# A hybrid Fourier, attention and expert layer on one core: each expert weight chunk rounded and subtracted whole, not in two halves

## The chip, the core and the metric

The kernel runs on one core of a Trainium2 chip. The metric is the device time of one execution in microseconds, of the median of the runs.

## The reference

One layer over a sequence of 1024 tokens of width 1024, all in float32. A mixing sub-layer (Fourier branch, grouped attention, gates, output projection) is followed by a routed feed-forward sub-layer with 32 experts, of which each token takes four. The change lies in this second one:

```python
def expert_block(args):
    e, rows = args
    xb = xf[rows]
    h = xb @ w_gate_up[e] + b_gate_up[e]
    gate, up = h[:, :D_EXPERT], h[:, D_EXPERT:]
    gate = jnp.minimum(gate, SWIGLU_LIMIT)
    up = jnp.clip(up, -SWIGLU_LIMIT, SWIGLU_LIMIT)
    act = (up + 1.0) * gate * jax.nn.sigmoid(SWIGLU_ALPHA * gate)
    return act @ w_down[e] + b_down[e]
```

`w_gate_up[e]` is 1024 x 2048 and `w_down[e]` 1024 x 1024, so the 32 experts' weights are 402 MB, each read once.

## The kernel before

TensorE multiplies float32 numbers here as pairs of rounded ones. A weight `w` becomes `whi`, the rounded value, and `wlo`, what the rounding left over (`w - whi`); the activations (`xTa`, `xTb`, `aTa`, `aTb`) are split in the same way. A product is then the sum of three matmuls (high by high, high by low, low by high; L141 to L143, L1140 to L1144), or of two where both parts of the activation stand side by side (L1184 and L1185, L1219 and L1220). ACT rounds (L147) and DVE subtracts (L148), both in the helper `split` (L145).

After the first sub-layer, the router and the placing of tokens comes the expert stage, from about 1090 to 2790 us of the span. The experts are ranked by their load; the fourteen fullest (up to 416 tokens) form lane a, which keeps weights stationary and puts tokens in the columns (`cols`, PSUM tile `psg`, and `psd` on the way down); the others (up to 128 or 64 tokens) form lane b, which keeps tokens stationary (`rows`, PSUM tile `psr`). `moe_plan` (L64) writes the order in which steps of the two lanes take turns, by estimated times. In lane b two chunks make one step pair, so the usual turn on TensorE is two short chunks of b and one longer of a.

Each expert has 12 chunks of weights, 1 MB each: eight of gate and up, four of down; 32 x 12 = 384 chunks. `load_chunk` (L1009) gets one: SP issues one or two DMAs into `wraw` (128 x 2048), and then `split` makes `whi` and `wlo`. Each of the three tiles has three buffers (pool `pew`, L1045), and a `Stream` (L1069) calls `load_chunk` two chunks ahead. A `wraw` buffer is free for the next load when DVE has subtracted; `whi` and `wlo` are free when TensorE has done with the chunk. The order of a chunk in `wraw` is by rows of the weight, so the first half of the tile holds the rows that the first matmuls of the chunk use, and these can start when the first half is split.

DVE and ACT have more to do in the stage: they take results out of PSUM (`gu`, `gur`, `xya`, `xyb`), compute the gated unit (`sgg`, `av`) and split activations (`aTa`, `aTb`, `xTa`, `xTb`). Every engine works its instructions in a fixed order. A scheduler in the build settles this order, by times that it assumes for each instruction; so a change of sizes also moves instructions.

Of the kernel before, what the change touches and what calls it, by code (L numbers as in the profile page):

```python
# [37 lines left out]
CAPS = [416, 320, 288, 288, 256, 256, 240, 208, 208, 192, 192, 160, 160, 160] + 7 * [128] + 11 * [64]  # L38

RANK_AT = 6  # L40
HALVES = [(0, 4), (4, 8)]
N_BIG = sum(n > P for n in CAPS)
LANE_A = [9, 0, 4, 1, 5, 2, 6, 3, 7, 8, 10, 11, 12, 13]
LANE_B = list(range(NE - 1, N_BIG - 1, -1))
# [62 lines left out]
def layer_kernel(ctx, tc, x, c, w_ada, b_ada, w_in, q_norm_g, k_norm_g, w_fourier, w_attn_o, w_out,  # L107
# [37 lines left out]
    def split(raw, hi, lo, lo_eng=None):  # L145

        act.activation(hi, raw, AF.Copy)  # L147
        (lo_eng or vec).tensor_tensor(lo, raw, f32(hi), op=ALU.subtract)  # L148
        return hi, lo
# [859 lines left out]
    def load_chunk(pl, wgu, wdn, i, wide=True, after=None):  # L1009
# [15 lines left out]
        with tc.issue_after(after.ins) if after else nullcontext():  # L1025
            for a, b in HALVES:
                split(raw[:, a:b, :], hi[:, a:b, :], lo[:, a:b, :])
# [456 lines left out]
```

## Time and profile before

| what | value |
|---|---|
| median of 3 runs | 2825.12 us (2825.11 to 2833.14) |
| the profiled execution | 2837.53 us, its span 2835.8 us |
| PE busy in the span | 2547.5 us (90%) |
| DVE busy | 2103.1 us (74%) |
| ACT busy | 1415.0 us (50%) |
| moved by DMA | 557.04 MB, mean 196 GB/s |

The profile is of one execution. Busy times of PE are of pipelined matmuls, so a busy PE is not PE at its peak; the idle time between them is what other engines and the clock leave to be won. PEld is the load of weights into TensorE, which goes ahead of the matmul; a wait for weights is seen there first.

### The profile page before, as it was taken

What the parts mean: (1) busy time and instruction counts of PE and PEld (TensorE: products, weight loads), DVE (VectorE), ACT (ScalarE), POOL (GpSimd) and SP (SyncE); (2) the same over time, 40 slices, a digit from 0 to 9 for tenths busy, and PEclk for the clock granted to TensorE, in tenths of its full rate; (3) what the DMA queues carried; (4) which work ended last, traced back from release to release, by engine and by line L of the source; (5) the groups of instructions that cost most, each with busy time, mean ns of one, the idle gap of its engine ahead of it and who ended that gap; (6) DMA issues with size and microseconds to landing.
All of it is one profiled execution on the core that took longest, in us unless ns stands there. A gap on an engine that the chain in (4) does not pass through costs nothing. (4 is left out here: it accounts for less than half of the span.)

```text
span 2835.8 us, 43042 instructions
## 1 busy us (share of the span) xinstructions
PE 2547.5 (90%) x15948; PEld 2308.4 (81%) x15948; DVE 2103.1 (74%) x3676; ACT 1415.0 (50%) x2174; POOL 412.2 (15%) x311
## 2 busy tenths in 40 slices
PE   6999999899999845889999999998999999998991
PEld 5888899799888834789889888986898888897881
DVE  7543338777755775878688888878897888887885
ACT  3411122466621533646466566656664665665662
POOL 3100002111031542000200010111101000120003
PEclk9999999999999957899999999999999999999996
DMA  6164420000054236767888798978988898988774
GB/s 227 57 195 152 152 66 16 16 1 1 1 186 134 68 112 215 252 212 244 244 272 281 249 293 268 299 228 267 309 264 258 265 295 272 301 274 267 240 252 151
DMA packets 466439, 557.04 MB, mean 196 GB/s; under 512 B 26377, under 2 KB 404689, under 8 KB 466177
## 3 DMA queue, kind: packets, MB, share of 16 engines
q1 hardware_dynamic: 448672, 494.41, 53.2%
q0 software_dynamic: 16464, 55.44, 7.4%
q10 hardware_dynamic: 1088, 4.39, 0.5%
q8 instruction: 127, 2.08, 0.3%
q14 instruction: 88, 0.71, 0.1%
HBM read 512.90 MB, written 42.62 MB: 196 GB/s over the span
## 5 line engine op out<-in xcount | busy, mean ns | idle before, releaser
L148 DVE TENSOR_TENSOR wlo<-wraw,whi 128x1024 fp32r<-128x1024 f32 x768 | 910.5, 1217 | 215.9 <-ACT whi L147 207.0
L147 ACT ACTIVATE whi<-wraw 128x1024 fp32r<-128x1024 f32 x768 | 768.5, 1051 | 462.5 <-DMA wraw<-in_w_gate_up_dram 155.3
L1144 PE MATMUL psg<-xTa,wlo 128*128 128x160 f32 (+7 forms) x1792 | 470.9, 278 | 1.6 <-DVE wlo L148 1.5
L1144 PEld LDWEIGHTS psg<-xTa,wlo 128*128 128x128 f32 x1792 | 342.5, 194 | 5.4 <-DVE wlo L148 3.3
L1140 PE MATMUL psg<-xTa,whi 128*128 128x320 f32 (+3 forms) x1024 | 308.7, 369 | 14.7 <-ACT whi L147 11.2
L141 PE MATMUL psd<-whi,aTa 128*128 128x256 f32 (+2 forms) x768 | 221.1, 292 | 27.8 <-ACT aTa L1168 14.9
L1142 PE MATMUL psg<-xTa,whi 128*128 128x256 f32 (+3 forms) x768 | 231.6, 306 | 8.7 <-ACT whi L147 7.5
L1143 PE MATMUL psg<-xTa,whi 128*128 128x256 f32 (+3 forms) x768 | 230.7, 304 | 0.0
L143 PE MATMUL psd<-whi,aTa 128*128 128x256 f32 (+2 forms) x768 | 217.3, 288 | 2.8 <-DVE aTa L1169 2.8
L142 PE MATMUL psd<-wlo,aTa 128*128 128x256 f32 (+2 forms) x768 | 218.1, 287 | 0.2 <-DVE wlo L148 0.2
L1140 PEld LDWEIGHTS psg<-xTa,whi 128*128 128x128 f32 x1024 | 197.0, 195 | 24.7 <-ACT whi L147 13.7
L141 PEld LDWEIGHTS psd<-whi,aTa 128*128 128x128 f32 (+2 forms) x768 | 146.1, 191 | 36.3 <-ACT aTa L1168 18.0
L1142 PEld LDWEIGHTS psg<-xTa,whi 128*128 128x128 f32 x768 | 146.5, 191 | 12.4 <-ACT whi L147 8.7
L1006 POOL DMA_INDIRECT acc_d<-xya,tab x33 | 60.9, 1847 | 649.7 <-DVE xya L1231 544.0
L143 PEld LDWEIGHTS psd<-whi,aTa 128*128 128x128 f32 (+2 forms) x768 | 145.6, 191 | 4.2 <-DVE aTa L1169 3.5
L142 PEld LDWEIGHTS psd<-wlo,aTa 128*128 128x128 f32 (+2 forms) x768 | 146.4, 191 | 1.6 <-DVE wlo L148 0.8
L1143 PEld LDWEIGHTS psg<-xTa,whi 128*128 128x128 f32 x768 | 146.7, 191 | 1.4
L1184 PE MATMUL psr<-whi,xTb 128*128 128x512 f32 x352 | 143.4, 407 | 4.3 <-ACT whi L147 4.2
L1185 PE MATMUL psr<-wlo,xTb 128*128 128x512 f32 x352 | 144.6, 411 | 2.0 <-DVE wlo L148 2.0
L147 ACT ACTIVATE wh<-wraw 128x1024 fp32r<-128x1024 f32 (+1 forms) x35 | 48.2, 1377 | 154.6 <-PE psg L206 93.1
L152 ACT ACTIVATE pth<-pst 128x512 fp32r<-128x512 f32 x128 | 75.0, 598 | 86.6 <-PE pst L632 85.3
L141 PE MATMUL pz<-wh,uh 128*128 128x256 f32 x384 | 110.5, 288 | 2.4 <-DVE mrow L480 2.4
(471 smaller groups left out, 6450.1 us busy)
## 6 DMA issues: line engine op xcount, KB each, us to landing
wraw<-in_w_gate_up_dram SPq DMA_DIRECT2D x512, 512.0 KB, 5.3
wraw<-in_w_down_dram SPq DMA_DIRECT2D x128, 1024.0 KB, 5.3
wa<-in_w_ada_dram SPq DMA_DIRECT2D x24, 1024.0 KB, 7.3
wraw<-in_w_in_dram SPq DMA_DIRECT2D x13, 1024.0 KB, 6.2
xs<-in_x_dram SPq DMA_DIRECT2D x8, 512.0 KB, 8.7
m_d<-sgm POOLq DMA_DIRECT2D x8, 512.0 KB, 5.7
sa_d<-sgm POOLq DMA_DIRECT2D x8, 512.0 KB, 3.2
wraw<-in_w_attn_o_dram SPq DMA_DIRECT2D x8, 512.0 KB, 3.6
```

The costliest lines, as they stand in the source:

```text
L141: pe_.matmul(o, lh, rh, start=start, stop=False)
L142: pe_.matmul(o, lh, rl, start=False, stop=False)
L143: pe_.matmul(o, ll, rh, start=False, stop=stop)
L147: act.activation(hi, raw, AF.Copy)
L148: (lo_eng or vec).tensor_tensor(lo, raw, f32(hi), op=ALU.subtract)
L152: act.activation(hi, ps, AF.Copy)
L1140: pe_.matmul(ps[:, :2 * n], wh[:, k, cs], xT[:, 4 * h + k, :, :], start=first, stop=False)
L1142: pe_.matmul(ps[:, :n], wh[:, k, cs], xh, start=first, stop=False)
L1143: pe_.matmul(ps[:, :n], wh[:, k, cs], xl, start=False, stop=False)
L1144: pe_.matmul(ps[:, :n], wl[:, k, cs], xh, start=False, stop=last)
L1184: pe_.matmul(o, xk, wh[:, k, :], start=False, stop=False)
L1185: pe_.matmul(o, xk, wl[:, k, :], start=False, stop=last)
```

## The change

The list of parts in which `load_chunk` splits a chunk has one entry instead of two. ACT rounds the whole chunk by one instruction, and DVE subtracts it by one.

```diff
-HALVES = [(0, 4), (4, 8)]
+HALVES = [(0, 8)]
```

It is used in one place (L1026):

```python
for a, b in HALVES:
    split(raw[:, a:b, :], hi[:, a:b, :], lo[:, a:b, :])
```

No tile, buffer, DMA or matmul is added or taken away. The scheduler gives another order, though. On DVE, in the middle of the stage (expert of lane a with 256 tokens, one of b with 64), before; `wlo_15436` and `wlo_15461` are two chunks of lane b, `gur` and `av1` belong to the gated unit of lane b, `sgg`, `aTa` and `gu` to lane a:

```order
L1194 TENSOR_TENSOR gur_15449<-psr_15402,gur_15449 64x512
L148 TENSOR_TENSOR wlo_15436<-wraw_15432,whi_15435 128x1024
L1038 TENSOR_SCALAR gur_15449<-gur_15449 64x256
L1039 TENSOR_SCALAR gur_15449<-gur_15449 64x256
L148 TENSOR_TENSOR wlo_15436<-wraw_15432,whi_15435 128x1024
L1162 TENSOR_TENSOR sgg_15392<-gu_15389,sgg_15392 128x256
L1041 SCALAR_TENSOR_TENSOR gur_15449<-gur_15449 64x256
L148 TENSOR_TENSOR wlo_15461<-wraw_15457,whi_15460 128x1024 x2
L1042 TENSOR_TENSOR av1_9761<-av1_9761,gur_15449 64x256
L1169 TENSOR_TENSOR aTa_15212<-sgg_15392,aTa_15212 128x2x128
```

The same place after, where `wlo_15436` is called `wlo_15186` and `wlo_15461` is `wlo_15209`:

```order
L1194 TENSOR_TENSOR gur_15197<-psr_15154,gur_15197 64x512
L148 TENSOR_TENSOR wlo_15186<-wraw_15182,whi_15185 128x2048
L1162 TENSOR_TENSOR sgg_15144<-gu_15141,sgg_15144 128x256
L1038 TENSOR_SCALAR gur_15197<-gur_15197 64x256
L1039 TENSOR_SCALAR gur_15197<-gur_15197 64x256
L1041 SCALAR_TENSOR_TENSOR gur_15197<-gur_15197 64x256
L148 TENSOR_TENSOR wlo_15209<-wraw_15205,whi_15208 128x2048
L1169 TENSOR_TENSOR aTa_14972<-sgg_15144,aTa_14972 128x2x128
L1042 TENSOR_TENSOR av1_9761<-av1_9761,gur_15197 64x256
```

The two steps on `gur` that stood between the halves of a chunk now stand behind the whole chunk's subtraction, with the step on `sgg` ahead of them. In the whole program 120 chunks had other DVE work between their halves, 167 instructions; now none has.

On PE, some 10 us later, before; `psr` is lane b's sum (its chunk is `whi_15569`, `wlo_15570`), `psg` lane a's (its chunk is `whi_15647`, `wlo_15648`), and L1205 is a transpose of lane b's activations:

```order
L1184 MATMUL psr_15643<-whi_15569,xTb_15168 128x512
L1185 MATMUL psr_15643<-wlo_15570,xTb_15168 128x512
L1184 MATMUL psr_15643<-whi_15569,xTb_15168 128x512
L1185 MATMUL psr_15643<-wlo_15570,xTb_15168 128x512
L1184 MATMUL psr_15643<-whi_15569,xTb_15168 128x512
L1205 MATMUL ptr_15869<-ident_63,av1_9761 128x128 x2
L1142 MATMUL psg_15696<-xTa_14756,whi_15647 128x256
L1143 MATMUL psg_15696<-xTa_14756,whi_15647 128x256
L1142 MATMUL psg_15697<-xTa_14756,whi_15647 128x256
L1143 MATMUL psg_15697<-xTa_14756,whi_15647 128x256
L1185 MATMUL psr_15643<-wlo_15570,xTb_15168 128x512
L1184 MATMUL psr_15643<-whi_15569,xTb_15168 128x512
```

The same place after, where the chunk of lane b is `whi_15311`, `wlo_15312` and that of lane a `whi_15387`, `wlo_15388`:

```order
L1184 MATMUL psr_15383<-whi_15311,xTb_14930 128x512
L1142 MATMUL psg_15430<-xTa_14530,whi_15387 128x256
L1143 MATMUL psg_15430<-xTa_14530,whi_15387 128x256
L1142 MATMUL psg_15431<-xTa_14530,whi_15387 128x256
L1143 MATMUL psg_15431<-xTa_14530,whi_15387 128x256
L1185 MATMUL psr_15383<-wlo_15312,xTb_14930 128x512
L1184 MATMUL psr_15383<-whi_15311,xTb_14930 128x512
L1185 MATMUL psr_15383<-wlo_15312,xTb_14930 128x512
```

Four matmuls of lane a that read its `whi` have moved from the chunk's middle to behind its first matmul on `whi`, and lane b's first matmul on `wlo` comes after them; the transpose has moved to a later place.

## Rows read from the trace of the kernel before

**Rows 1.** The page, busy us (share of the span) and instructions of each engine.

```profile
PE 2547.5 (90%) x15948; PEld 2308.4 (81%) x15948; DVE 2103.1 (74%) x3676; ACT 1415.0 (50%) x2174; POOL 412.2 (15%) x311
```

**Rows 2.** Busy time by window, the expert stage; columns in the first row.

```profile
core 0: us, PE busy (x) PEld busy (x) DVE busy (x) ACT busy (x) POOL busy (x), PEclk, DMA share, GB/s
1090.00:2790.00 1700.00, 1573.14 (x9912) 1439.52 (x9912) 1393.39 (x2286) 1015.50 (x1521) 173.69 (x98) 0.97 0.82 261
```

**Rows 3.** Waits of the weight loads, expert stage: us in total, times, longest us.

```profile
PEld psg L1140 <- ACT whi L147: 13.7, 7, 5.2
...
PEld psr L142 <- DVE wlo L148: 6.0, 8, 1.1
...
PEld psr L1184 <- ACT whi L147: 5.9, 5, 3.0
...
PEld psd L142 <- DVE wlo L148: 0.8, 2, 0.5
```

**Rows 4.** Waits of the weight loads for other results, same view.

```profile
PEld psd L141 <- ACT aTa L1168: 18.0, 10, 5.4
...
PEld psr L1180 <- DVE xyb L1231: 0.8, 1, 0.8
```

**Rows 5.** Groups of instructions: busy us, mean ns of one, idle before; whole span.

```profile
L148 DVE TENSOR_TENSOR wlo<-wraw,whi 128x1024 fp32r<-128x1024 f32 x768 | 910.5, 1217 | 215.9 <-ACT whi L147 207.0
L147 ACT ACTIVATE whi<-wraw 128x1024 fp32r<-128x1024 f32 x768 | 768.5, 1051 | 462.5 <-DMA wraw<-in_w_gate_up_dram 155.3
```

**Rows 6.** The same view for 0 to 1090 us: the shape 128x2048.

```profile
L148 DVE TENSOR_TENSOR wl<-wraw,wh 128x2048 fp32r<-128x2048 f32 x13 | 29.8, 2289 | 29.4 <-ACT wh L147 29.3
...
L147 ACT ACTIVATE wh<-wraw 128x2048 fp32r<-128x2048 f32 x13 | 24.9, 1913 | 82.4 <-PE psg L206 74.8 <-DMA wraw<-in_w_in_dram 7.6
```

**Rows 7.** Timeline, one chunk: start us, us, engine, line, operation [idle before <-releaser].

```profile
1671.90 2.00 ACT L147 ACTIVATE whi<-wraw 128x1024 fp32r<-128x1024 f32 x2 [2.96 <-DMA wraw<-in_w_gate_up_dram]
...
1672.99 2.36 DVE L148 TENSOR_TENSOR wlo<-wraw,whi 128x1024 fp32r<-128x1024 f32 x2 [1.85 <-ACT whi L147]
...
1673.02 0.50 PE L1184 MATMUL psr<-whi,xTb 128*128 128x512 f32 x1 [0.94 <-ACT whi L147]
1674.27 0.51 PE L1185 MATMUL psr<-wlo,xTb 128*128 128x512 f32 x1 [0.76 <-DVE wlo L148]
1674.62 0.40 PE L1184 MATMUL psr<-whi,xTb 128*128 128x512 f32 x1
1674.85 0.40 PE L1185 MATMUL psr<-wlo,xTb 128*128 128x512 f32 x1
...
1675.41 0.68 PE L1185 MATMUL psr<-wlo,xTb 128*128 128x512 f32 x1
...
1676.31 0.63 PE L1185 MATMUL psr<-wlo,xTb 128*128 128x512 f32 x1
```

**Rows 8.** Timeline, TensorE: first use of the first and of the last late chunk.

```profile
1104.57 0.97 PE L1140 MATMUL psg<-xTa,whi 128*128 128x384 f32 x4 [0.91 <-ACT whi L147]
...
2758.43 0.49 PE L141 MATMUL psr<-whi,aTb 128*128 128x512 f32 x1 [1.15 <-ACT whi L147]
```

**Rows 9.** Timeline, DVE: other work between the two halves of a subtraction.

```profile
1678.91 1.23 DVE L148 TENSOR_TENSOR wlo<-wraw,whi 128x1024 fp32r<-128x1024 f32 x1
1680.06 0.28 DVE L1038 TENSOR_SCALAR gur<-gur 64x256 f32<-64x256 f32 x1
...
1680.46 1.21 DVE L148 TENSOR_TENSOR wlo<-wraw,whi 128x1024 fp32r<-128x1024 f32 x1
```

**Rows 10.** Waits of all engines, 1100 to 2750 us: us in total, times, longest us.

```profile
DVE wlo L148 <- ACT whi L147: 206.7, 148, 7.2
...
ACT whi L147 <- DMA wraw<-in_w_gate_up_dram: 152.2, 95, 8.1
```

**Rows 11.** Waits of SP's queue, whole span, same columns.

```profile
SPq L1018 <- DVE wlo L148: 291.6, 112, 9.2
```

**Rows 12.** The page, DMA issues: count, KB each, median us to landing.

```profile
wraw<-in_w_gate_up_dram SPq DMA_DIRECT2D x512, 512.0 KB, 5.3
```

## Prediction

> **What bounds the kernel now.** I read the page's engine shares first, then one window over the expert stage, then who TensorE waits for in it, and last single chunks in the timeline. The page gives TensorE 90% of the span, DVE 74%, ACT 50% [rows 1]. Everything that changes lies in the expert stage, 1090 to 2790 us: there PE is busy 1573 of 1700 us, DVE 1393, ACT 1016, the DMA engines 82%, and the granted clock averages 0.97 [rows 2]. [...]
>
> What TensorE's weight loads wait for in the stage: for `whi` (ACT's rounding) in five rows, 24 waits, 43.5 us; for `wlo` (DVE's subtraction) in five rows, 26 waits, 16.3 us; the first and the last row of each are in [rows 3]. For other results of ACT and DVE (`aTa`, `xya`, `xTa`, `gur`, `av` ...) there are fourteen rows, 55 waits, 80 us, of which the first and the last are in [rows 4]. So a split that comes late already costs PE, and evictions that come late cost more.
>
> **The change, what the engines do.** 384 chunks are split, each by two ACT and two DVE instructions of 128x1024; that is the x768 of [rows 5], 1.05 and 1.22 us each. After it, one of 128x2048 on each engine. The trace has this very shape elsewhere: `wh` 1.91 us on ACT, `wl` 2.29 us on DVE, 13 of each [rows 6]. Two halves back to back take 2.00 us on ACT and 2.36 on DVE [rows 7], so a pair costs only 0.09 and 0.07 more than a whole: 384 x 0.07 = 27 us of DVE time and 384 x 0.09 = 35 us of ACT time go away.
>
> What it adds is latency. In halves, DVE starts 1.1 us after ACT did, and the first half of `wlo` is there at about 2.3 us, the second at 3.45 (1671.90 to 1675.35, [rows 7]). In one piece `whi` is there after 1.91 and `wlo` after 1.91 + 0.04 + 2.29 = 4.24 us. So the first half of `whi` comes 0.86 us later, the first half of `wlo` 1.93 later, the raw buffer comes free 0.8 later.
>
> **Term 1, chunks that TensorE takes at once.** [Rows 7] is such a chunk: PE takes `whi` at 1673.02, 0.06 after its first half is done, idles, takes `wlo` at 1674.27, idles again until 1675.41 for the second half. With the whole, `wlo` comes at 1671.90 + 4.24 + 0.06 = 1676.20, 1.93 later, but the third wait is gone: the first matmul on `wlo` and six more at the 0.23 us pitch (1674.62 to 1674.85) follow without a stop, the last ends near 1676.20 + 6 x 0.23 + 0.40 = 1678.0, and before it ended at 1676.94. So the chunk ends about 1.1 later and not 1.93: a factor 0.57. I set each of the 384 chunks' ACT start (and DVE start, where DVE was busy) beside the first matmul that reads its `whi` and `wlo`, and asked how late the whole would be. 91 chunks are hit, from the one that PE takes at 1104.57 to the one at 2758.43 [rows 8], with 93 us in all at the first use; 25 us of that is from `whi` alone, which is the lower end. By the factor it is 53 us. 29 of the 91 (34 us) had their split started by TensorE freeing a buffer; their delay isn't made good, because the next split of that buffer starts later too: 34 x 0.57 = 19. The other 62 (59 us) waited for a load or for ACT. A TensorE that is behind gives them slack, while the later release of the raw buffer takes it away; I take half, 59 x 0.57 / 2 = 17. Term 1: 36 us, between 14 (25 x 0.57) and 93.
>
> **Term 2, evictions behind a longer subtraction.** In 120 chunks the order of before has other DVE work, 167 instructions, between the two halves; in the order of after there is none (the first excerpt). [Rows 9] is such a place: steps of 0.28 us between two subtractions. An instruction that becomes ready while DVE is subtracting waits up to 1.07 us longer (2.29 - 1.22), on average half of that, and DVE subtracts about half the time (768 subtractions, 910.5 us of [rows 5], nearly all in these 1700 us). So 55 waits [rows 4] x 0.54 x 0.53 = 16 us; bounds 0 and 55 x 1.07 = 59. Queued behind it are the evictions that free PSUM (`psr` has one buffer) and TensorE waits for these. I take 13, since the scheduler puts some of the 167 ahead of the subtraction rather than behind.
>
> **Term 3, what is saved.** The 27 us of DVE time are worth something only where PE waits for DVE's queue. I take 12 of it; bounds 0 and 27. ACT has 684 us of idle time in the stage [rows 2]: nothing.
>
> [...]
>
> Sum: 36 + 13 - 12 + 7 = 44, say +45 us. The profiled execution took 2837.5 us (span 2835.8), 12.4 above the median of 2825.1; I add the difference to the median: 2870 us, +1.6%. The scheduler softens it too: in the second excerpt it no longer lets `wlo` follow `whi` but puts four matmuls of the next chunk between them. That is in the factor and the halving of term 1.
>
> [...]
>
> **Rivals.**
> *Faster: DVE's queue is the bound.* Place: stretches in which DVE runs behind ACT, so that the subtraction starts 1.95 us or more after ACT did. This holds for 63 chunks; there the whole ends 0.07 earlier than the halves. Price: the 27 us, and with them up to a third of the 80 us of [rows 4] would go: -15 to -27, around 2805 us. It decides if the scheduler's new order hides the late `wlo` behind the other lane's matmuls in most of the 91 chunks. For it: 293 of 384 chunks have slack enough. Against it: DVE waited 207 us in 148 places for `whi` [rows 10], so its queue was often empty, not full. [...]
>
> *Hidden: no change that can be told.* 293 chunks have slack, the delays of the 62 are made good, and the saved DVE time pays for the rest: +14 + 0 - 12 = about +2 us, 2827.
>
> *Larger: the ring of raw buffers becomes the bound.* Three raw buffers; each goes round by a load of 5.3 us [rows 12] and a split of 3.45 us, 8.8 us for three chunks, against the stage's mean of 1700 x 3 / 384 = 13.3. With 4.24 it is 9.6. SP's load issues already wait for `wlo`, 291.6 us in 112 places in one row [rows 11], and ACT waits for loads, 152.2 us in 95 places [rows 10]. If each chunk paid its third of the 0.8 us: 384 x 0.26 = 101 us, about 2926. Against it: 13.3 is well above 9.6; only runs of short chunks (64 rows, about 2 us each) come near.
>
> *The change doesn't do what it says.* The order of after has one ACT and one DVE instruction of 128x2048 for each chunk, so I give this nothing.
>
> **How the numbers follow.** Forecast (+0.3% to about +3.5%) 0.54, ring 0.14, hidden 0.15, faster 0.17. About 0.3% is what a measurement of this kernel can tell from no change. Slower is 0.54 + 0.14 = 0.68, same 0.15, faster 0.17. Range: the lowest sum, 14 + 0 - 27 = -13, gives 2812, and the ring 2926; half of the faster case and half of the ring's lie outside 2810 to 2930, about 0.16.
>
> **What would show it.** Right: `wlo` x384 at 2.29 and `whi` x384 at 1.91 us; DVE's busy time in the stage down by 27 to 60 us (single instructions don't overlap as pairs do) and PE's idle time up from 127 to about 165; the waits of weight loads for `wlo` up from 16 to 40 us or more, at over 1 us each; the granted clock of the stage below 0.97. Wrong: waits for `wlo` as before (the scheduler hid it), or PE idle below 127 us (then DVE was the bound). If loads are the most frequent releaser of ACT with far more than 152 us, the ring has it.

## The result

| | before | after |
|---|---|---|
| median | 2826.6 us (2825.1 to 2833.1, 4 runs) | 2904.1 us (2899.6 to 2919.0, 4 runs) |
| profiled execution, span | 2835.8 us | 2917.2 us |

The ratio of the times is 1.027, with a 95% interval of 1.0227 to 1.0313: the change makes the kernel slower by 77 us. The forecast was 2870 us, so the sign was right and the size too small by 34 us.

The page of the changed kernel, first the engines' busy times, then the two groups that the change made (busy us, mean ns of one, idle time before with what ended it), to be read beside [rows 1] and [rows 5]:

```profile
PE 2570.7 (88%) x15948; PEld 2317.2 (79%) x15948; DVE 2075.9 (71%) x3292; ACT 1381.5 (47%) x1790; POOL 406.5 (14%) x311
...
L148 DVE TENSOR_TENSOR wlo<-wraw,whi 128x2048 fp32r<-128x2048 f32 x384 | 876.1, 2286 | 310.5 <-ACT whi L147 301.0
L147 ACT ACTIVATE whi<-wraw 128x2048 fp32r<-128x2048 f32 x384 | 732.6, 1914 | 534.7 <-DMA wraw<-in_w_gate_up_dram 161.1
```

The instructions are as foreseen, 2.29 and 1.91 us. DVE's busy time fell by 2103.1 - 2075.9 = 27 us and ACT's by 34, just what the pairs cost above a whole. Nobody gained by it: DVE now stands idle ahead of its subtraction for 310.5 us instead of 215.9.

The expert stage ends 80 us later. The window over it (same columns as [rows 2]):

```profile
core 0: us, PE busy (x) PEld busy (x) DVE busy (x) ACT busy (x) POOL busy (x), PEclk, DMA share, GB/s
1090.00:2870.00 1780.00, 1596.48 (x9916) 1448.29 (x9916) 1370.14 (x1916) 982.88 (x1142) 168.11 (x100) 0.96 0.79 250
```

PE's idle time in the stage is 1780 - 1596 = 184 us, 57 more than the 127 of before. PE's busy time rose too, by 23 us for the same matmuls, while the granted clock went from 0.97 to 0.96. 57 + 23 = 80 us: that is nearly all of the 81 us by which the spans of the two profiled executions differ. Some 5 us of it lie ahead of the first expert chunk, whose first matmul starts at 1103.3 instead of 1097.8 us; from there to the last matmul on an expert chunk it is 1758 us instead of 1682, 76 more.

What the weight loads wait for in the stage (us in total, times, longest us), to be read beside [rows 3] and [rows 4]:

```profile
PEld psr L142 <- DVE wlo L148: 29.3, 20, 2.1
PEld psg L1144 <- DVE wlo L148: 22.4, 24, 2.0
PEld psr L1180 <- DVE gur L1194: 19.7, 10, 6.1
PEld psd L141 <- ACT aTa L1168: 19.3, 8, 5.4
PEld psr L141 <- ACT whi L147: 13.7, 13, 2.7
PEld psr L1185 <- DVE wlo L148: 10.3, 10, 2.1
...
PEld psg L1140 <- ACT whi L147: 8.5, 6, 2.8
```

All rows of each kind added up (the prediction's 80 us and 55 waits for other results leave out one of 4.1 us, for `novi`, which belongs to the placing of tokens; in the last row I leave out a wait of 7.2 us at L1275 of the same placing, since before it lies at 1087 us, ahead of the window, with 6.5 us):

| weight loads wait for | before | after |
|---|---|---|
| `wlo` | 16.3 us, 26 waits | 72.2 us, 67 waits |
| `whi` | 43.5 us, 24 waits | 37.5 us, 29 waits |
| other results of ACT and DVE | 83.7 us, 56 waits | 93.8 us, 49 waits |

(These are waits of the loads, which run ahead of the matmuls, so not all of them is idle time of PE: in the chunk below its load waits 1.00 us for `wlo`, where PE is idle for 0.58.) The waits for `wlo` are mostly not due to a DVE that is busy elsewhere: by the trace, DVE began the subtraction over 0.1 us after `whi` was there in 28 of the 67, and at most 11 of the 72 us go with that. A chunk of lane a, at 1708 us, by the timeline (start us, us, engine, line, operation):

```profile
1708.36 1.92 ACT L147 ACTIVATE whi<-wraw 128x2048 fp32r<-128x2048 f32 x1 [0.19 <-DMA wraw<-in_w_gate_up_dram]
...
1710.17 0.28 DVE L1038 TENSOR_SCALAR gur<-gur 64x256 f32<-64x256 f32 x1
1710.37 0.28 DVE L1039 TENSOR_SCALAR gur<-gur 64x256 f32<-64x256 f32 x1
1710.58 0.41 DVE L1160 SCALAR_TENSOR_TENSOR gu<-gu 128x256 f32<-128x256 f32 x1
1710.91 2.27 DVE L148 TENSOR_TENSOR wlo<-wraw,whi 128x2048 fp32r<-128x2048 f32 x1
...
1710.33 0.39 PE L1142 MATMUL psg<-xTa,whi 128*128 128x256 f32 x1 [0.43 <-ACT whi L147]
...
1710.90 0.39 PE L1185 MATMUL psr<-wlo,xTb 128*128 128x512 f32 x1
...
1713.24 0.38 PE L1144 MATMUL psg<-xTa,wlo 128*128 128x256 f32 x1 [0.58 <-DVE wlo L148]
```

PE waits for the whole of `whi`, does four matmuls with it, fills in with seven of lane b (the new order of the second excerpt), and still has to wait for `wlo`. The scheduler's filling hides part of the delay and not all of it: of the 2.91 us from the first matmul on `whi` to the first on `wlo` (1710.33 to 1713.24) PE is idle for 0.58. This chunk is one of the 28: `whi` was there at 1710.28, and DVE, which had another chunk's subtraction until 1710.24 and then did three steps for other results, began 0.63 us later. That is about as much as PE's last wait, 0.58 us.

### The profile page after: what moved, and what is told of

It is laid out like the page before. It is cut to its first block, busy times and chain, and to the rows that moved or that the text cites. A ratio compares the mean times of both kernels' runs of the same rounds, so it can differ in the third digit from the quotient of the medians.

```text
span 2917.2 us, 42268 instructions
## 1 busy us (share of the span) xinstructions
PE 2570.7 (88%) x15948; PEld 2317.2 (79%) x15948; DVE 2075.9 (71%) x3292; ACT 1381.5 (47%) x1790; POOL 406.5 (14%) x311
## 5 line engine op out<-in xcount | busy, mean ns | idle before, releaser
L148 DVE TENSOR_TENSOR wlo<-wraw,whi 128x2048 fp32r<-128x2048 f32 x384 | 876.1, 2286 | 310.5 <-ACT whi L147 301.0
L147 ACT ACTIVATE whi<-wraw 128x2048 fp32r<-128x2048 f32 x384 | 732.6, 1914 | 534.7 <-DMA wraw<-in_w_gate_up_dram 161.1
L141 PE MATMUL psd<-whi,aTa 128*128 128x256 f32 (+2 forms) x768 | 218.4, 288 | 29.4 <-ACT aTa L1168 16.9
L143 PE MATMUL psd<-whi,aTa 128*128 128x256 f32 (+2 forms) x768 | 213.9, 283 | 4.9 <-DVE aTa L1169 4.9
L142 PE MATMUL psd<-wlo,aTa 128*128 128x256 f32 (+2 forms) x768 | 215.9, 283 | 1.4 <-DVE wlo L148 1.3
L141 PEld LDWEIGHTS psd<-whi,aTa 128*128 128x128 f32 (+2 forms) x768 | 143.2, 187 | 37.5 <-ACT aTa L1168 19.3
L1142 PEld LDWEIGHTS psg<-xTa,whi 128*128 128x128 f32 x768 | 146.3, 191 | 13.3 <-ACT whi L147 6.7
L1185 PE MATMUL psr<-wlo,xTb 128*128 128x512 f32 x352 | 147.0, 418 | 6.4 <-DVE wlo L148 6.3
L143 PEld LDWEIGHTS psd<-whi,aTa 128*128 128x128 f32 (+2 forms) x768 | 142.4, 187 | 6.2 <-DVE aTa L1169 5.5
L142 PE MATMUL psr<-wlo,xTb 128*128 128x512 f32 x224 | 94.7, 423 | 20.6 <-DVE wlo L148 20.6
```

The costliest lines, as they stand in the source:

```text
L141: pe_.matmul(o, lh, rh, start=start, stop=False)
L142: pe_.matmul(o, lh, rl, start=False, stop=False)
L143: pe_.matmul(o, ll, rh, start=False, stop=stop)
L1142: pe_.matmul(ps[:, :n], wh[:, k, cs], xh, start=first, stop=False)
L1185: pe_.matmul(o, xk, wl[:, k, :], start=False, stop=last)
```

## The experiments

The kernel before was measured again beside each group of experiments, on the same chip; its median was 2832.2 us beside the kernels of the first part below, 2826.8 beside those with less room, and 2833.9 beside the last four. Each ratio is to the one beside it. In the expectations L is the theory of the piece that comes late, R that of the raw buffers, D that of DVE's queue; L2 and D2 are second forms of two of them, given where they first stand.

### One part alone, the other end first, smaller parts

ACT whole, DVE in halves:

```diff
-            for a, b in HALVES:
-                split(raw[:, a:b, :], hi[:, a:b, :], lo[:, a:b, :])
+            act.activation(hi, raw, AF.Copy)
+            for a, b in HALVES:
+                vec.tensor_tensor(lo[:, a:b, :], raw[:, a:b, :], f32(hi[:, a:b, :]), op=ALU.subtract)
```

> ACT rounds the chunk whole, DVE still subtracts in halves. Theory L (TensorE stands still because the first piece of a chunk that it needs comes later): the first half of whi comes 0.86 us later, the first half of wlo 0.86 later (3.2 instead of 2.3 us after ACT's start) instead of the 1.93 of the change, so about 0.45 of the 77 us: +25 to +45 us. Rival D (evictions queue behind a DVE instruction of 2.29 instead of 1.22 us): DVE's instructions keep their size, 0 to +10 us. Rival R (raw buffers come free 0.8 us later): they come free at 4.3 us as in the change, +70 to +80 us.

Measured: 2914.1 us, ratio 1.0284 (1.0257 to 1.0311), +82 us of 2832.2. As much as the change itself. Theory L (+25 to +45) and rival D as it is worded (0 to +10) miss: DVE's instructions are as short as before (1.22 us each), and the loss is there. Rival R's figure is the nearest. But here too hardly any other DVE work stands between the halves (11 chunks by the trace, against 117 before), so this run does not speak against the order on DVE.

ACT in halves, DVE whole:

```diff
-            for a, b in HALVES:
-                split(raw[:, a:b, :], hi[:, a:b, :], lo[:, a:b, :])
+            for a, b in HALVES:
+                act.activation(hi[:, a:b, :], raw[:, a:b, :], AF.Copy)
+            vec.tensor_tensor(lo, raw, f32(hi), op=ALU.subtract)
```

> ACT rounds in halves, DVE subtracts the chunk whole. Theory L: whi is on time, but the first piece of wlo comes 2.0 us later (4.3 instead of 2.3), as in the change; since the waits for whi did not grow in the change, nearly the full loss: +60 to +80 us. Rival D: +70 to +80 us, DVE's instructions are as long as in the change. Rival R: +70 to +80 us. This run only tells that ACT's part is or isn't needed; if it is, less than +50 us.

Measured: 2909.1 us, ratio 1.0267 (1.0242 to 1.0293), +77 us. Either part alone brings the whole loss. The two have one thing in common with the change: the last half of `wlo` is there 4.31 and 4.33 us after ACT's start in the median chunk (4.25 in the change), against 3.81 before, where the best chunks have 3.45. What the first half does differs: in the one ACT rounds in halves as before (1.05 us each), in the other `wlo` comes about 1 us sooner than in the change (an estimate from single instructions, 1.91 + 0.04 + 1.22 = 3.17 against 4.24 us).

The second half first:

```diff
-HALVES = [(0, 4), (4, 8)]
+HALVES = [(4, 8), (0, 4)]
```

> Two halves as before, but the second half of the chunk is split first. Instructions, their sizes and the release of the raw buffer (3.45 us) are those of before; only the half that the first matmuls read comes second: whi 0.95 us later, wlo 1.15 us later. Theory L: 0.6 of the 77 us, +35 to +60 us. Rival D and rival R: within 0.3% of before, -8 to +8 us.

Measured: 2825.9 us, ratio 0.9976 (0.9961 to 0.9991), no loss. This is the run that my own theory failed: the half that PE needs first is late by about as much as with ACT whole (0.95 and 1.15 us against 0.86, by the estimates above), and it costs nothing. The waits of the weight loads show that it is late all the same:

```profile
PEld psg L1144 <- DVE wlo L148: 14.1, 16, 2.2
PEld psr L142 <- DVE wlo L148: 13.5, 15, 1.9
```

All waits for `wlo` are 42.7 us there (16.3 before), but those for `whi` and for other results fell by 9 and 18 us, and PE's idle time in the stage is no longer than before (205 us in the window from 1090 to 2870 us, 207 before). So a wait at the first use seems to be made good where the chunk's end does not move (in the mean the last `wlo` is there 4.21 us after ACT's start, 4.20 before).

Four parts:

```diff
-HALVES = [(0, 4), (4, 8)]
+HALVES = [(0, 2), (2, 4), (4, 6), (6, 8)]
```

> Four parts instead of two. The first quarter of wlo is there at about 1.35 us instead of 2.3, the last at about 3.3; DVE gets about 384 x 2 x 0.07 = 54 us more work, ACT about 70. Theory L: waits for wlo of the weight loads fall from 16 towards 5 us and those for whi from 43 to about 33; -10 to -25 us if DVE's extra work stays off the path. Rival D: shorter instructions, so evictions come sooner, -5 to -15 us. If DVE's busy time itself is the bound: +20 to +55 us.

Measured: 2837.5 us, ratio 1.0019 (1.0005 to 1.0033): no gain. DVE is busy for 2144.8 us of the span instead of 2103.1, 42 more, and PE's waits for splits stay at 64 us against 60. Smaller first pieces bring nothing, in line with the run before this; what DVE's and ACT's additional work took from it is not told apart.

### A fourth raw buffer, with less room for the fullest experts

To make room for a fourth `wraw`, four runs have the room of the fullest experts cut (`CAPS`), by which some tokens are left out:

```diff
+ROOM = CAPS
+CAPS = [min(n, 256) for n in CAPS]
...
-"t_cap": np.array([CAPS], np.float32)
+"t_cap": np.array([ROOM], np.float32)
```

and the fourth buffers, for expert chunks alone (the last of these kernels has `bufs=nb` on `whi` and `wlo` as well):

```diff
-    def load_chunk(pl, wgu, wdn, i, wide=True, after=None):
+    def load_chunk(pl, wgu, wdn, i, wide=True, after=None, nb=3):
...
-        raw = pl.tile([P, KT, 256], F32, name="wraw")
+        raw = pl.tile([P, KT, 256], F32, name="wraw", bufs=nb)
...
-                return load_chunk(pew, *reg["w"], i, r >= N_BIG, tail[0] if (r, i) in plan[:3] else None)
+                return load_chunk(pew, *reg["w"], i, r >= N_BIG, tail[0] if (r, i) in plan[:3] else None, 4)
```

The kernel before and the change, with three buffers:

> Control for three runs with other buffer counts: the kernel before, with the room of the four fullest experts cut to 256 tokens, to make space in SBUF; the tokens beyond are left out (so this computes less). About 90 us less work for TensorE: 2730 to 2760 us.

Measured: 2739.0 us.

> The change with the same cut (the same tokens left out). All theories: as far above b256 as the change is above the kernel before, or somewhat more since TensorE has less work to hide it: +70 to +100 us.

Measured: 2811.2 us, 72 us above b256. The loss is there in this smaller kernel as well.

> The change with the same cut and a fourth buffer for wraw, so that a load can start one chunk earlier. Theory R (the load waits for the raw buffer that comes free 0.8 us later): nearly all of the loss comes back, b256 +0 to +20 us. Theory L2 (TensorE can't finish a chunk before its last piece is there, 4.25 instead of 3.45 us after the split's start, whatever starts the split): about the half that waits for loads, b256 +35 to +60 us. Theory D2 (no eviction can go between the two halves on DVE any more): nothing comes back, b256 +70 to +100 us.

Measured: 2741.0 us, 2 us above b256. By this run alone the load ring would have it all; it lacked the control, the kernel before with a fourth buffer, which the pair at full size below has.

> The change with the same cut and a fourth buffer for wraw, whi and wlo, so that the whole split starts one chunk earlier. Theory L2: the split's 4.25 us lie ahead of TensorE and most comes back, b256 -10 to +25 us. Theory R: the same as with the fourth raw buffer alone, b256 +0 to +20 us. Theory D2: nothing comes back, b256 +70 to +100 us, since DVE's order is as in the change.

Measured: 2771.2 us, 32 us above b256 and 30 worse than the fourth raw buffer alone. No theory foresaw that. With more room for `whi` and `wlo` the waits for `wlo` are longer (two lines more stand above, so L150 is L148):

```profile
PEld psg L1146 <- DVE wlo L150: 47.5, 28, 5.7
PEld psd L144 <- DVE wlo L150: 23.5, 12, 3.2
PEld psr L144 <- DVE wlo L150: 17.2, 12, 2.6
```

The order in which the scheduler put the instructions may be the reason: by the traces, 2951 of the 9520 matmuls of the stage stand outside the longest order that this kernel and b256 have in common, against 1330 for a256. I have no run that takes the order apart from the buffers, and none of the kernel before with the same buffers, so this one settles nothing; that an order is worth some 30 us is a guess from it.

### A raw buffer held longer

```diff
                 split(raw[:, a:b, :], hi[:, a:b, :], lo[:, a:b, :])
+            rest = pl.tile([P, 3, 256], F32, name="rest", bufs=1)
+            act.activation(rest, raw[:, 4:7, :], AF.Identity, scale=f32(lo)[:, 7, 255:256])
```

In the control, `raw[:, 4:7, :]` is `f32(lo)[:, 4:7, :]`.

> The kernel before, halves and all, with one more ACT instruction per chunk of 128x768 (about 0.83 us): it reads part of wraw and waits for the second half of wlo, so the raw buffer comes free 0.8 us or more later, while whi and wlo are ready as before. Read against hold_lo, which has the same instruction on wlo. Theory R (the round of a raw buffer sets the pace: load, split, next load): hold_lo +50 to +90 us. Theory L2 (what counts is when TensorE has the whole chunk): hold_lo -10 to +10 us.

> Control for hold_raw: the same additional ACT instruction, at the same place and with the same wait, but it reads wlo and not wraw, so no raw buffer is held. ACT gets 384 x 0.83 = 320 us more work (60 to 78% of the stage): +0 to +60 us over the kernel before by either theory, since evictions on ACT wait for it.

Measured: hold_raw 2949.4 us, ratio 1.0408 (1.0377 to 1.0439); hold_lo 2834.1 us, ratio 1.0001 (0.9985 to 1.0016). The same instruction, at 0.93 us each and 357 us in all on ACT, costs nothing when it reads `wlo`, and 115 us when it reads `wraw`, more than theory R's +50 to +90. The scheduler gave the two kernels different orders too (1441 of the 9912 matmuls of the stage stand outside their longest common order), so the 115 us are not shown to be the held buffer alone. SP's queue of hold_raw shows who now holds the loads, beside [rows 11]:

```profile
SPq L1018 <- ACT rest L1029: 512.2, 140, 10.7
...
SPq L1020 <- ACT rest L1029: 132.5, 31, 8.5
...
SPq L1022 <- ACT rest L1029: 87.2, 25, 11.5
```

and ACT's waits for loads, of hold_raw:

```profile
ACT whi L147 <- DMA wraw<-in_w_gate_up_dram: 218.4, 131, 8.2
```

and of hold_lo:

```profile
ACT whi L147 <- DMA wraw<-in_w_gate_up_dram: 75.7, 55, 7.5
```

In hold_raw a load is issued 2.7 us after the end of the chunk's subtraction (mean of the 381 chunks after the first three), in the kernel before 0.1 us after. The waits for loads are 143 us longer than in hold_lo. So the time for which a raw buffer is held is on the path in the kernel before: 115 / 2.6 = about 45 us for each microsecond, as an estimate. In the change the split takes 0.55 us longer (mean from ACT's start to the last end of `wlo`, 4.75 against 4.20 us; by the traces, 0.2 us longer in the 159 chunks where DVE began over 1.4 us after ACT in the kernel before, and 0.8 in the other 225). At that price it would be 25 us of the 77, if the price also holds for a smaller delay.

### A fourth raw buffer at full size

One `av` buffer and one `sel` less make the space; nothing is left out. The edit of `load_chunk` is that of the kernels above.

```diff
-        avs = [pes.tile([P, D], F32, name=f"av{i}") for i in range(2)]
+        avs = [pes.tile([P, D], F32, name=f"av{i}") for i in range(1)]
...
-                    self.sel = pe.tile([P, P], F32R, name="sel")
+                    self.sel = pe.tile([P, P], F32R, name="sel", bufs=1)
...
-                    self.av = avs[self.r % 2]
+                    self.av = avs[0]
```

> The change at full size with a fourth wraw buffer; one av buffer instead of two and one sel instead of two make the space. Theory R: the loss of 77 us is gone, and with less work on DVE and ACT it comes to -20 to +10 us against the kernel before. Theory L2: half of it is left, +30 to +50 us. One av buffer may cost up to 15 us in either.

Measured: 2848.3 us, ratio 1.0055 (1.0038 to 1.0072), +14 us: above theory R's range and below L2's.

> The kernel before, in halves, with the same fourth wraw buffer and the same cuts of av and sel: control for a_raw4. If three raw buffers already bound the kernel before (theory R in the strong form), it gains 20 to 60 us against the kernel before and a_raw4 is within 15 us of it. If they did not, it is within 0.5% of the kernel before. If a_raw4 is 60 us or more above this run, a fourth raw buffer doesn't undo the change's loss and theory R falls.

Measured: 2789.9 us, ratio 0.9855 (0.9824 to 0.9885): faster than both kernels, by 44 us against the one before. Three raw buffers did bind the kernel before. But the change still loses 2848.3 - 2789.9 = 58 us, just short of the 60 at which I had wanted to give up theory R. So a fourth buffer takes about 19 of the 77 us (by the intervals of the three ratios give or take some 15), not at odds with the 25 worked out above, and the rest is not in the loads. ACT's waits for gate and up loads are down to the same 36.5 us in both (152.2 before), first of a_raw4, then of b_raw4:

```profile
ACT whi L147 <- DMA wraw<-in_w_gate_up_dram: 36.5, 29, 4.1
```

```profile
ACT whi L147 <- DMA wraw<-in_w_gate_up_dram: 36.5, 27, 5.1
```

The median chunk lies in its raw buffer for over 5 us in both before ACT begins (5.8 and 5.4 by the traces, 1.7 before). What ACT waits for instead is TensorE: all rows of `whi` behind a matmul, which frees a buffer of `whi`, come to 354 us in 181 waits in a_raw4 and 307 in 173 in b_raw4 (257 in 127 before); the longest row of each:

```profile
ACT whi L147 <- PE psd L1219: 78.5, 21, 12.1
```

```profile
ACT whi L147 <- PE psg L1143: 61.2, 33, 8.1
```

A split that starts when TensorE frees a buffer, and for which TensorE then waits, may be a round of its own, which a longer split would make longer; no run here tests it cleanly (the kernel with a fourth buffer of `whi` and `wlo` had no control). The page's first rows tell where the 58 us are, a_raw4 and then b_raw4: PE is 20 us longer busy with the same matmuls, and the rest, 38 us, is idle time. Some 8 us lie ahead of the first expert chunk; from its first matmul to the last one on an expert chunk it is 1687 us in a_raw4 and 1637 in b_raw4, 50 more, against the 76 with three raw buffers. Why the stage is entered later was not tested.

```profile
PE 2545.0 (89%) x15948; PEld 2301.6 (81%) x15948; DVE 2077.8 (73%) x3292; ACT 1380.5 (49%) x1790; POOL 428.5 (15%) x310
```

```profile
PE 2524.9 (91%) x15948; PEld 2289.7 (82%) x15948; DVE 2101.0 (75%) x3676; ACT 1413.9 (51%) x2174; POOL 406.0 (15%) x310
```

With most of the waits for loads out of the way the weight loads of a_raw4 wait 25 us longer for `wlo` than those of b_raw4 (38.5 against 13.0), 5 longer for `whi` and 5 longer for other results (84.4 against 79.2, again without the wait at L1275, which falls into the window in a_raw4 alone). Rows of a_raw4:

```profile
PEld psr L1180 <- DVE gur L1194: 20.0, 13, 3.8
PEld psr L142 <- DVE wlo L148: 19.4, 15, 2.1
PEld psg L1144 <- DVE wlo L148: 12.5, 12, 2.1
```

## Why the prediction was right in sign and short in size

**What bounds the kernel**: with PE busy for 1573 of the 1700 us of the stage [rows 2], the loss came out of its idle time, 127 to 184 us (foreseen: about 165), and of its longer busy time, 23 us, at a granted clock of 0.96 instead of 0.97. The signs came as named (67 waits for `wlo`, 1.1 us each; granted clock 0.96; DVE's busy time in the stage 23 us less, a little short of the 27 to 60), but the sign for the ring misled: ACT's waits for gate and up loads went only from 155.3 [rows 5] to 161.1 us, by which the ring was to have no part, and the runs show that it has one.

**Term 1, late chunks** (36 us, bounds 14 and 93): the weight loads' waits for `whi` and `wlo` together went from 60 to 110 us, +50. Within that, 25 of the 93 us were to come from `whi` alone, and the waits for `whi` fell by 6. The step that failed is the last one. I had 53 us for the 91 chunks, and then halved the share of the 62 whose split waits for a load or for ACT, since a PE that is behind would give them slack. It does not, as far as the runs show: the raw buffer comes free later as well, and hold_raw (115 us above hold_lo) and b_raw4 (44 us below the kernel before) show that its release is on the path. The halving took off 17 us; the pair with a fourth raw buffer puts some 19 on the raw buffers. Without the halving the term is 53, close to what the waits show. The other half of its reasoning was off in a way that did not show in the number: I counted from the first use of `wlo`, and reversed shows that a late first piece by itself costs nothing here (ratio 0.9976). What the slower kernels share is a later last piece (4.75 to 4.84 us after ACT's start in the mean for the change, act_whole, dve_whole and a_raw4, against 4.12 to 4.28 for before, reversed, quarters, hold_lo and b_raw4); the factor 0.57, which turns 1.93 us at the first use into 1.1 at the chunk's end, brought the term near, and that it did so is partly luck.

**Term 2, evictions** (13 us, bounds 0 and 59): waits for other results rose from 84 to 94 us, +10. About right as a number. The mechanism as I gave it, a longer instruction in the way, can't be what does it in act_whole, where the instructions are short (1.22 us) and these waits are 106 us. That the order on DVE does it was not shown: no run keeps the two halves and forbids other work between them. The full-size kernels with nothing or next to nothing between the halves (the change, act_whole, dve_whole, a_raw4; 0 to 11 chunks) have 84 to 106 us of such waits, those with work between them in 112 to 204 chunks by the traces (before, reversed, quarters, hold_lo, b_raw4) 66 to 84 (all without the wait at L1275), and hold_raw, which has it too, 88. Among the cut kernels it isn't so (b256 79, a256 72 us).

**Term 3, what is saved** (12 us): the 27 us on DVE and 34 on ACT were saved as foreseen, but the waits for other results, which that was to shorten, are longer (84 to 94 us), and nothing ties the 6 us less for `whi` to it. In hold_lo 357 us more work on ACT cost nothing that can be told (ratio 1.0001). No run isolates the gain; the lower bound, 0, fits what they show.

**Term 4, the clock** (7 us): no run shows this term; the 7 us, a price in clock for more idle time, were my estimate. What the runs show in its place is that PE was busy for 23 us more with the same matmuls, while the granted clock of the stage went from 0.97 to 0.96. Whether either comes from the idle time was not tested. I also had 36 + 13 - 12 = 37 us of more idle time instead of 57.

By its own steps without the halving in term 1, the sum would have been 53 + 13 - 12 = 54 us of idle time, against the 57 that came; without the 12 us of gain, 66. That the first figure is near the measured one is partly luck, since the 53 counts from a first use that does not count.

**The rivals.** The ring of raw buffers, with a chance of 0.14, was a part of the truth: it did bind the kernel before (b_raw4 gains 44 us), and carries, by two estimates with wide errors, some 19 to 25 of the 77 us. My argument against it was that 13.3 us of the stage for three chunks is well above the ring's 9.6. That compared means; the chunks come in unequal steps, and the rows of [rows 10] (95 waits for loads) said so. Its own price, 101 us, took all of 0.8 us for all chunks and was too high. "Faster" fell: DVE had 27 us less to do and PE was idle for 57 us more. "Hidden" fell with it.

What stays open: of the 58 us that are left with four raw buffers, how much is the later end of each split, how much the evictions that can't go between the halves, and how much the order that the scheduler gave. In all full-size kernels that lose, hold_raw aside, the first two go together. For the first: of the weight loads' additional waits in a_raw4 the larger part is for `wlo` (25 of 35 us), and by the trace DVE's late start accounts for at most 7 of the 38.5. For the order no run is a test, but reordering as such need not cost: by the traces, 1250 of the 9912 matmuls of the stage stand outside the longest common order of the change and the kernel before (those of the same tiles and size counted in turn), and 941 in hold_lo, 993 in reversed and 1479 in quarters, which are within 0.3% of the kernel before. Which matmuls move may still matter, as a256_all4 leaves one to suspect.

DVE is busy for 82% of the stage [rows 2], and joining the halves cost 77 us. That halves work by the first piece being there sooner is not what these runs show (reversed); the later end of the last piece is what all the slower kernels of that kind have in common. A further split gained nothing (quarters, 1.0019). A whole does cost less busy time than a pair (27 us less on DVE, 34 on ACT), but that tells nothing of the kernel's time here, +77 us.

## What to carry to other kernels

Where tiles go round through a few buffers, ask first when the last piece of a step ends and each buffer comes free, not only when the first piece is there. Here a late first piece alone cost nothing (reversed, 0.9976), and the four full-size kernels whose split ended 0.5 us or more later in the mean lost 58 to 82 us against the like kernel in halves, though how much of that the later end itself cost is open. Time saved on an engine that has idle time in the stage (27 us on DVE, 34 on ACT) was worth nothing that could be seen here; a delay may be worth its full price even where the means suggest slack. Test a ring by an instruction that only holds the buffer, with a control that reads something else, and then by one buffer more for both kernels, not for the changed one alone.

## What was not expected of the hardware

In hold_lo ACT did 357 us more work in the span (384 instructions of 0.93 us) without any change of the time that can be told, ratio 1.0001 (0.9985 to 1.0016). And two subtractions of 128x1024 back to back took 2.36 us [rows 7], only 0.07 more than one of 128x2048, 2.29 [rows 6], though the profile gives a single one 1.22 [rows 5]: the sum of durations overstates what splitting an instruction costs, here 0.15 against 0.07 us.
